# Seven half-size products in place of eight for 18 of 22 gate/up tiles of one SwiGLU sublayer

## The chip, the cores and the metric

The program runs on one core of one Trainium2 chip. The metric is the device time of one execution in microseconds; the kernel before takes 1680.61 us as the median of 3 runs (1678.48 to 1683.15). TensorE (PE) multiplies, VectorE (DVE), ScalarE (ACT) and GpSimd (POOL) work on what lies in the on-chip memories, and the queue of SyncE (SP) issues the loads.

## The reference

A two-layer backbone works on 256 latent tokens `x` and 256 context tokens `z`, with 1024 features. Each layer is a SwiGLU sublayer, a token mixer (a gated short convolution in layer 0, windowed attention in layer 1) and a second SwiGLU sublayer; all are in float32.

```python
def rmsnorm(x, g):
    y = x * lax.rsqrt(jnp.mean(x * x, axis=-1, keepdims=True) + RMS_EPS)
    return y * g

def swiglu(h, w_gu, w_down):                    # h [256, 1024], w_gu [1024, 2 * 2816], w_down [2816, 1024]
    gu = h @ w_gu
    return (jax.nn.silu(gu[..., :D_FF]) * gu[..., D_FF:]) @ w_down

def ffn_sublayer(x, mod, k, g_pre, g_post, w_gu, w_down):
    h = rmsnorm(x, g_pre) * (1 + mod[k + 1]) + mod[k]
    return x + 0.5 * mod[k + 2] * rmsnorm(swiglu(h, w_gu, w_down), g_post)

for i in range(2):
    mx = silu(c) @ w_mod[i] + b_mod[i]          # 9 vectors of 1024 coefficients; mz the same from c_ctx
    x = ffn_sublayer(x, mx, 0, ..., ffn_w_gu[i, 0], ffn_w_down[i, 0])
    z = ffn_sublayer(z, mz, 0, ..., ffn_w_gu[i, 0], ffn_w_down[i, 0])
    ...                                         # mixer, then the second SwiGLU sublayer
```

The change is in layer 1's first SwiGLU (`ffn_w_gu[1, 0]`), which both streams pass.

## The kernel before

The layout is feature-major: an activation is a row of tiles of 128 features by 512 tokens, the latent 256 tokens (slice `X`) in front of the context 256 (slice `Z`). A float32 product is carried by three fp32r products of split operands: each operand is cut into `hi` and `lo`, and hi*hi, lo*hi and hi*lo are summed in PSUM (L398, L399, L400, in `groups`). So each 128x128 weight tile costs three weight loads and three matmuls; a matmul streams 512 tokens ("128x512") or one stream's half of them ("128x256").

Weights come from DRAM in slots of 8 tiles, 128x1024 float32. `load` (L232 on) issues the slot's load on SP (L238) into a ring `raw` of 3 buffers, ACT copies it into `whi` (L243), and DVE, or POOL for the slots listed in `POOL`, subtracts to get `wlo` (L244). `whi` and `wlo` are rings of 8.

A SwiGLU sublayer (`ffn`) has 22 feature tiles, taken in three chunks. In a chunk, `gate_up` works out each feature tile: 8 weight tiles for gate and 8 for up, then ACT takes silu of gate (L436), DVE multiplies by up from PSUM (L438), and `hilo` splits the result into `ah` (ACT, L408) and `al` (DVE, L409). Then `project` multiplies the chunk's tiles by the down weights into `y` (8 output tiles; later chunks are added on DVE, L459). The first four tiles of the sublayer, the heads (`HEADS`), run for the latent half first and then for the context half, woven with the norms of the sublayer before; the norm chain of a half writes the new `h` as `hh` (ACT, L372) and `hl` (DVE, L373) from `ut` (DVE, L371, one input in PSUM).

The modulation vectors are worked out on DVE in between, as dots of 128x1024 (`dot`, L297) on weights that come through the same SP queue into two buffers `wmd`. The sublayer of the change carries 24 of them for one stream.

PE runs its instructions in the order of the program. The order on ACT, DVE, POOL and SP is set by a scheduler, and each engine takes its instructions in that order, so an instruction that waits holds all that stand behind it. The sublayer lies at about 961 to 1313 us of the profile.

Of the kernel before, what the change touches and what calls it, by code (L numbers as in the profile page):

```python
# [32 lines left out]
CHUNKS = {0: ((0, 7), (7, 14), (14, 22)), 2: ((0, 7), (7, 14), (14, 22)), 3: ((0, 7), (7, 14), (14, 22))}  # L33
# [5 lines left out]
# feature tiles of the first two adaLN chunks: by dots, by pairs; and the loads ahead of the first product (latent  # L39
# and context stream, tiles for dots, tiles of pairs, weights)  # L40
# [4 lines left out]
RAW = 3  # L45
# [52 lines left out]
def ffn_slots(w_gu, w_down, chunks):  # L98
# [3 lines left out]
    for a, b in chunks:  # L102
        out.append(slots_of(np.stack([gu[a:b], gu[FT + a:FT + b]], 1).reshape(-1, P, P)))
# [4 lines left out]
def lay_out(i):  # L108
# [9 lines left out]
    w += ffn_slots(i["ffn_w_gu"][1, 0], i["ffn_w_down"][1, 0], CHUNKS[3])  # L118
# [976 lines left out]
```

## Time and profile before

| | |
|---|---|
| median of 3 runs | 1680.61 us (1678.48 to 1683.15) |
| profiled execution, first to last instruction (its own time) | 1676.8 us |
| PE busy | 1642.4 us, 98% of the span |
| DVE, ACT, POOL busy | 1048.6, 644.0, 265.3 us |
| mean granted TensorE clock | 0.994 |
| DMA | 246.73 MB, mean 147 GB/s |

The profiled execution's own time is known only as its span, which lies 3.8 us below the median of the timed runs; the difference is what lies around the first and last instruction and between executions. PE's busy time is modelled from starts, so the pace of PE is better read from the starts of its matmuls. DVE's 63% is an average over stages that load it very differently.

### The profile page before, as it was taken

What the parts mean: (1) busy time and instruction counts of PE and PEld (TensorE: products, weight loads), DVE (VectorE), ACT (ScalarE), POOL (GpSimd) and SP (SyncE); (2) the same over time, 40 slices, a digit from 0 to 9 for tenths busy, and PEclk for the clock granted to TensorE, in tenths of its full rate; (3) what the DMA queues carried; (4) which work ended last, traced back from release to release, by engine and by line L of the source; (5) the groups of instructions that cost most, each with busy time, mean ns of one, the idle gap of its engine ahead of it and who ended that gap; (6) DMA issues with size and microseconds to landing.
All of it is one profiled execution on the core that took longest, in us unless ns stands there. A gap on an engine that the chain in (4) does not pass through costs nothing.

```text
span 1676.8 us, 23525 instructions
## 1 busy us (share of the span) xinstructions
PE 1642.4 (98%) x9378; PEld 1419.1 (85%) x9378; DVE 1048.6 (63%) x1570; ACT 644.0 (38%) x1051; POOL 265.3 (16%) x192
## 2 busy tenths in 40 slices
PE   8999999999999999999999999999999999989998
PEld 3788888889988998888888998888888997889987
DVE  7779779856644375977965564344443679665553
ACT  4532322325432643322232543222222558654442
POOL 1100000125102430000110521000000664130000
PEclk9999999999999999999999999999999999999999
DMA  8557556543322224655655224444433221045551
GB/s 317 188 164 237 189 187 217 194 156 102 101 89 101 68 71 165 213 188 165 219 191 166 80 74 148 160 132 150 153 124 114 94 89 64 26 160 198 194 192 50
DMA packets 70306, 246.73 MB, mean 147 GB/s; under 512 B 7730, under 2 KB 10290, under 8 KB 70196
## 3 DMA queue, kind: packets, MB, share of 16 engines
q1 hardware_dynamic: 69908, 245.02, 44.3%
q8 instruction: 73, 1.20, 0.3%
q14 instruction: 37, 0.30, 0.1%
q10 hardware_dynamic: 288, 0.20, 0.0%
HBM read 244.15 MB, written 1.05 MB: 146 GB/s over the span
## 4 chain that ended last, share of the span: by engine, by line
PE 90%; DVE 5%; ACT 2%; POOL 1%; issue 1%; DMA 1%; SPq 0%; DVEq 0%; POOLq 0%; ACTq 0%
PE mm L399 27%; PE mm L398 27%; PE mm L400 27%; PE mm L925 1%; PE mm L926 1%; PE mm L924 1%; PE po L801 1%; DVE junk L297 1%; PE tp L787 1%; POOL acc L359 1%; PE mm L747 1%; DMA xr<-in_xz 1%; PE prb L318 0%; ACT whi L243 0%; DVE acc L360 0%
## 5 line engine op out<-in xcount | busy, mean ns | idle before, releaser
L398 PE MATMUL mm<-hh,whi 128*128 128x512 f32 (+1 forms) x1520 | 549.3, 361 | 4.3 <-ACT hh L408 4.0
L399 PE MATMUL mm<-hh,wlo 128*128 128x512 f32 (+1 forms) x1520 | 547.9, 360 | 0.0
L400 PE MATMUL mm<-hl,whi 128*128 128x512 f32 (+1 forms) x1520 | 543.1, 357 | 0.0
L243 ACT ACTIVATE whi<-raw 128x1024 fp32r<-128x1024 f32 x316 | 330.5, 1056 | 440.2 <-PE mm L400 372.4
L244 DVE TENSOR_TENSOR wlo<-raw,whi 128x1024 fp32r<-128x1024 f32 x260 | 325.8, 1261 | 203.3 <-ACT whi L243 202.2
L398 PEld LDWEIGHTS mm<-hh,whi 128*128 128x128 f32 x1520 | 285.8, 188 | 53.6 <-ACT hh L408 5.3
L400 PEld LDWEIGHTS mm<-hl,whi 128*128 128x128 f32 x1520 | 285.9, 188 | 45.0 <-DVE hl L409 0.6
L399 PEld LDWEIGHTS mm<-hh,wlo 128*128 128x128 f32 x1520 | 286.3, 188 | 41.3
L297 DVE CUSTOM_DVE_ANT_0 junk<-wmd,sc,vec 128x1024 bf16<-128x1024 f32 x232 | 304.7, 1313 | 17.0 <-DMA wmd<-in_wmd 13.2
L244 POOL TENSOR_TENSOR wlo<-raw,whi 128x1024 fp32r<-128x1024 f32 x56 | 140.1, 2507 | 1005.2 <-ACT whi L243 1001.5
L398 PE MATMUL mm<-ah,whi 128*128 128x256 f32 (+1 forms) x848 | 276.8, 326 | 0.0
L399 PE MATMUL mm<-ah,wlo 128*128 128x256 f32 (+1 forms) x848 | 276.0, 326 | 0.0
L400 PE MATMUL mm<-al,whi 128*128 128x256 f32 (+1 forms) x848 | 274.1, 323 | 0.0
L398 PEld LDWEIGHTS mm<-ah,whi 128*128 128x128 f32 x848 | 160.5, 189 | 14.9
L400 PEld LDWEIGHTS mm<-al,whi 128*128 128x128 f32 x848 | 160.5, 189 | 14.1
L399 PEld LDWEIGHTS mm<-ah,wlo 128*128 128x128 f32 x848 | 160.8, 190 | 12.7
L438 DVE TENSOR_TENSOR pr<-mm,sg 128x512 f32<-128x512 f32 (+1 forms) x96 | 56.1, 584 | 181.6 <-PE mm L400 127.5
L436 ACT ACTIVATE sg<-mm 128x512 f32<-128x512 f32 (+1 forms) x96 | 49.2, 513 | 301.7 <-PE mm L400 301.7
L399 PE MATMUL mm<-h,wlo 128*128 128x256 f32 x352 | 98.8, 281 | 0.0
L398 PE MATMUL mm<-h,whi 128*128 128x256 f32 x352 | 98.6, 280 | 0.0
L400 PE MATMUL mm<-h,whi 128*128 128x256 f32 x352 | 98.4, 280 | 0.0
L409 DVE TENSOR_TENSOR al<-pr,ah 128x512 fp32r<-128x512 f32 (+1 forms) x84 | 74.6, 888 | 13.3 <-ACT ah L408 13.2
(185 smaller groups left out, 1496.5 us busy)
## 6 DMA issues: line engine op xcount, KB each, us to landing
raw<-in_wst SPq DMA_DIRECT2D x316, 512.0 KB, 3.5
wmd<-in_wmd SPq DMA_DIRECT2D x140, 512.0 KB, 4.2
xr<-in_xz SPq DMA_DIRECT2D x2, 1024.0 KB, 9.8
wmq<-in_wmd SPq DMA_DIRECT2D x8, 256.0 KB, 7.8
out_y<-xt SPq DMA_DIRECT2D x3, 256.0 KB, 2.1
rtab<-in_cst SPq DMA_DIRECT2D x1, 512.0 KB, 3.6
out_y<-xt SPq DMA_DIRECT2D x2, 128.0 KB, 1.8
msk<-in_cst ACTq DMA_DIRECT2D x1, 192.0 KB, 4.0
```

The costliest lines, as they stand in the source:

```text
L243: nc.scalar.activation(hi, raw, AF.Copy)
L244: d = sub.tensor_tensor(lo, raw, hi.bitcast(F32), ALU.subtract)
L297: self.keep(self.nc.vector.tensor_tensor_reduce(junk, wt, self.sc[v], 1.0, b, ALU.mult, ALU.add, out))
L359: nc.gpsimd.tensor_tensor(acc, acc, sq, ALU.add)
L398: nc.tensor.matmul(pt[:, :n], whi, rhi[:, sl], start=i == 0, stop=False)
L399: nc.tensor.matmul(pt[:, :n], wlo, rhi[:, sl], start=False, stop=False)
L400: nc.tensor.matmul(pt[:, :n], whi, rlo[:, sl], start=False, stop=i == last)
L409: i = (sub or self.nc.vector).tensor_tensor(lo[:, sl], src, hi[:, sl].bitcast(F32), ALU.subtract)
L436: nc.scalar.activation(sg[:, :n], pg[:, :n], AF.Silu)
L438: self.keep(nc.vector.tensor_mul(pr[:, :n], pu[:, :n], sg[:, :n]))
L747: nc.tensor.matmul(sp[e], act[4 * p2 + 2 * jp + jj][x][rows[e], qs], kt[p2][w][rows[e], :], start=a == 0, stop=False)
L787: nc.tensor.transpose(tp[:, c * P:(c + 1) * P], pe[c][:, kc // 2, kc % 2 * P:(kc % 2 + 1) * P], self.ident)
```

## The change

In the sublayer `ffn(1, 0)`, index 3 of the lists, the chunks become 6, 8 and 8 tiles instead of 7, 7 and 8. Tiles 0 to 3 stay as they were; tiles 4 to 21 are taken by twos in the new method `pair`, nine pairs: one in chunk 0, four each in chunks 1 and 2. A pair takes the two feature tiles of gate and of up, and the first and second half of the 1024 input features, as a 2x2 block matrix of weights, and the latent and context streams as the other one; seven products of sums of blocks replace eight products of blocks. Each of the seven has 8 weight tiles and 256 tokens, so 24 matmuls of 128x256; a pair has 168 of these where two tiles had 96 of 128x512. PE's order is P1 of the next pair, P7 of this pair, P2 to P6 of the next pair.

The sums of weight blocks are made on DVE (`s3`, and three sums in place, 128x1024 each); each of the seven operands is split (`split`), the `lo` on DVE except for P4, P5 and P6 (`POOLED`), which go to POOL. The activation sums are made once, in `forms`, ahead of the first pair: `hh + hl` for the eight feature tiles (half on POOL), four combinations of 128x1024, and their splits. Three of them keep 3 of the 8 buffers of `whi` and `wlo` until the sublayer's last pair; the fourth overwrites the context half of `h[0]` to `h[3]`. `RAW` goes from 3 to 6, the ring `tmp` from 3 to 4.

```diff
-CHUNKS = {0: ((0, 7), (7, 14), (14, 22)), 2: ((0, 7), (7, 14), (14, 22)), 3: ((0, 7), (7, 14), (14, 22))}
+CHUNKS = {0: ((0, 7), (7, 14), (14, 22)), 2: ((0, 7), (7, 14), (14, 22)), 3: ((0, 6), (6, 14), (14, 22))}
+SEVEN = {3: 4}
+POOLED = (3, 4, 5)
-RAW = 3
+RAW = 6
...
+    def split(self, src, sub=None):
+        hi = self.ring.tile([P, SLOT * P], F32R, name="whi", tag="whi")
+        lo = self.ring.tile([P, SLOT * P], F32R, name="wlo", tag="wlo")
+        self.nc.scalar.activation(hi, src, AF.Copy)
+        (sub or self.nc.vector).tensor_tensor(lo, src, hi.bitcast(F32), ALU.subtract)
+        return hi, lo
...
+    def forms(self):
...
+        hf = self.cp.tile([P, KT, N], F32, name="hf", tag="y")
+        for k in (4, 0, 5, 1, 6, 2, 7, 3):
+            hi, lo = (t.bitcast(F32) for t in self.h[k])
+            (nc.gpsimd if k % 4 in (1, 3) else nc.vector).tensor_tensor(hf[:, k], hi, lo, ALU.add)
+        fx, fz, bx, bz = (hf[:, k:k + 4, h] for k in (0, 4) for h in (X, Z))
...
+        nc.vector.tensor_tensor(fx, fx, fz, ALU.subtract)
+        nc.vector.tensor_tensor(fz, bz, fz, ALU.subtract)
...
+    def pair(self, s, forms, act):
...
+        a11 = self.raw(s)
+        w = self.split(a11, gp(0))
+        ba = self.bank()
+        product(ba, w, b11, True)
+        yield
+        up = tmp("up", "tmp", bufs=4)
+        nc.scalar.activation(up, ba, AF.Copy)
+        a21 = self.raw(s + 1)
+        s3 = self.ring.tile([P, SLOT * P], F32, name="raw", tag="raw", bufs=RAW)
+        nc.vector.tensor_add(s3, a11, a21)
+        w = self.split(s3, gp(1))
+        a22 = self.raw(s + 2)
+        nc.vector.tensor_add(a21, a21, a22)
+        bb = self.bank()
+        product(bb, w, t3, True)
+        gz = tmp("gz", "tmp", bufs=4)
+        nc.scalar.activation(gz, bb, AF.Copy)
+        nc.vector.tensor_add(a11, a21, a11)
+        w = self.split(a11, gp(2))
+        product(ba, w, t2)
+        gx = tmp("gx", "sq")
+        nc.scalar.activation(gx, ba, AF.Copy)
+        a12 = self.raw(s + 3)
+        w = self.split(a12, gp(3))
+        bc = self.bank()
+        product(bc, w, b21, True)
+        nc.vector.tensor_add(up, up, bc)
+        w = self.split(a21, gp(4))
+        product(ba, w, t1)
+        nc.vector.tensor_add(gz, gz, ba)
+        nc.scalar.activation(gz, gz, AF.Silu, scale=-1.0)
+        w = self.split(a22, gp(5))
+        product(bb, w, t4)
+        nc.vector.tensor_add(gx, gx, bb)
+        nc.scalar.activation(gx, gx, AF.Silu, scale=-1.0)
+        nc.vector.tensor_add(a12, a11, a12)
+        w = self.split(a12, gp(6))
+        yield
+        product(ba, w, b22)
+        nc.vector.tensor_mul(up, up, gx)
+        nc.vector.tensor_mul(gz, gz, ba)
+        for m in range(2):
+            c = slice(m * S, (m + 1) * S)
+            for t, h in ((up, X), (gz, Z)):
+                hi, lo = act[m]
+                nc.scalar.activation(hi[:, h], t[:, c], AF.Copy)
+                nc.vector.tensor_tensor(lo[:, h], t[:, c], hi[:, h].bitcast(F32), ALU.subtract)
...
+            for m in range(max(m0, seven), nk, 2):
+                p = self.pair(base + 2 * m, forms, act[m:m + 2])
+                next(p)
+                for _ in last or ():
+                    pass
+                next(p)
+                last = p
+                pace(2 * PACE)
+            for _ in last or ():
+                pass
```

Outside the sublayer PE's order is the same. On ACT and DVE the order changes a little at the start of the program: on DVE two more weight splits now stand ahead of the first `hl` of tile 5 and three ahead of that of tile 7, and ACT's copies move up with them.

The first place is DVE in the norm chain of the context half, while the latent heads run. Before, from `hl` of feature tile 3 (`hl_7618`) to that of tile 7 (`hl_7626`):

```order
L373 SCALAR_TENSOR_TENSOR hl_7618<-ut,mod_0_1_5992,hh_7617 128x256
L371 SCALAR_TENSOR_TENSOR ut<-xr,mod_1_1_5687,prb 128x256 x2
L438 TENSOR_TENSOR pr<-mm,sg 128x256
L373 SCALAR_TENSOR_TENSOR hl_7620<-ut,mod_0_1_5992,hh_7619 128x256
L373 SCALAR_TENSOR_TENSOR hl_7622<-ut,mod_0_1_5992,hh_7621 128x256
L371 SCALAR_TENSOR_TENSOR ut<-xr,mod_1_1_5687,prb 128x256
L409 TENSOR_TENSOR al_8234<-pr,ah_8233 128x256
L371 SCALAR_TENSOR_TENSOR ut<-xr,mod_1_1_5687,prb 128x256
L373 SCALAR_TENSOR_TENSOR hl_7624<-ut,mod_0_1_5992,hh_7623 128x256
L373 SCALAR_TENSOR_TENSOR hl_7626<-ut,mod_0_1_5992,hh_7625 128x256
```

The same stretch of DVE in the changed kernel, where L398 is the line of `hl`, and L473 and L477 are lines of `forms`:

```order
L398 SCALAR_TENSOR_TENSOR hl_7618<-ut,mod_0_1_5992,hh_7617 128x256
L463 TENSOR_TENSOR pr<-mm,sg 128x256
L398 SCALAR_TENSOR_TENSOR hl_7620<-ut,mod_0_1_5992,hh_7619 128x256
L396 SCALAR_TENSOR_TENSOR ut<-xr,mod_1_1_5687,prb 128x256 x2
L473 TENSOR_TENSOR hf<-hh_7619,hl_7620 128x512
L434 TENSOR_TENSOR al_8234<-pr,ah_8233 128x256
L477 TENSOR_TENSOR hf<-hf 128x4x256
L398 SCALAR_TENSOR_TENSOR hl_7622<-ut,mod_0_1_5992,hh_7621 128x256
L398 SCALAR_TENSOR_TENSOR hl_7624<-ut,mod_0_1_5992,hh_7623 128x256
L396 SCALAR_TENSOR_TENSOR ut<-xr,mod_1_1_5687,prb 128x256
L473 TENSOR_TENSOR hf<-hh_7623,hl_7624 128x512
L398 SCALAR_TENSOR_TENSOR hl_7626<-ut,mod_0_1_5992,hh_7625 128x256
```

Sums of `forms` now stand between the rows of the chain (two more, of tiles 0 and 2, stand just above this piece), and the row at L477 waits for POOL's sums of tiles 1 and 3.

The second place is DVE at the end of chunk 0. Before, its last feature tile there (tile 6, `al_8240`), with the dots behind it (`mod_7_0` is the modulation vector that they fill):

```order
L438 TENSOR_TENSOR pr<-mm,sg 128x512
L244 TENSOR_TENSOR wlo<-raw,whi 128x1024
L409 TENSOR_TENSOR al_8240<-pr,ah_8239 128x512
L297 ISA junk,mod_7_0_8951<-wmd,sc_95,vec 128x1024
L297 ISA mod_7_0_8951 128x1
```

In the changed kernel, the end of chunk 0's one pair (tiles 4 and 5; L554 is the last product's gate, L560 the `al`):

```order
L543 TENSOR_TENSOR gz_8911<-gz_8911,mm_8848 128x512
L547 TENSOR_TENSOR gx_8942<-gx_8942,mm_8886 128x512
L553 TENSOR_TENSOR up_8873<-up_8873,gx_8942 128x512
L322 ISA junk_9277,mod1_7_0_9045<-wmd_9245,sc0_95,vec_79 128x1024
L322 ISA mod1_7_0_9045 128x1
L554 TENSOR_TENSOR gz_8911<-gz_8911,mm_8848 128x512
L560 TENSOR_TENSOR al4_8236<-up_8873,ah4_8235 128x256
L560 TENSOR_TENSOR al5_8238<-up_8873,ah5_8237 128x256
L322 ISA junk_9301,mod1_7_0_9045<-wmd_9275,sc0_95,vec_79 128x1024
L322 ISA mod1_7_0_9045 128x1
L254 TENSOR_TENSOR wlo_9223<-raw_9220,whi_9222 128x1024
L560 TENSOR_TENSOR al4_8236<-gz_8911,ah4_8235 128x256
```

One dot now stands between P7 and the product `gz*ba` that waits for it, and a dot and a weight split stand ahead of the context half's `al`.

The third place is DVE in chunk 1. Before, two tiles' worth of it (`al4`, `al5`):

```order
L438 TENSOR_TENSOR pr_9637<-mm_9574,sg_9635 128x512
L244 TENSOR_TENSOR wlo_9884<-raw_9881,whi_9883 128x1024
L409 TENSOR_TENSOR al4_9282<-pr_9637,ah4_9281 128x512
L297 ISA junk_9643,mod1_6_0_9430<-wmd_9569,sc0_95,vec_79 128x1024
L297 ISA mod1_6_0_9430 128x1
L244 TENSOR_TENSOR wlo_9917<-raw_9914,whi_9916 128x1024
L438 TENSOR_TENSOR pr_9709<-mm_9646,sg_9707 128x512
L244 TENSOR_TENSOR wlo_9950<-raw_9947,whi_9949 128x1024
L409 TENSOR_TENSOR al5_9284<-pr_9709,ah5_9283 128x512
```

In the changed kernel, from P7's operand of the chunk's first pair to the middle of the second pair:

```order
L549 TENSOR_TENSOR raw_9659<-raw_9523,raw_9659 128x1024
L523 TENSOR_TENSOR raw_9830<-raw_9761,raw_9828 128x1024
L554 TENSOR_TENSOR gz_9388<-gz_9388,mm_9325 128x512
L560 TENSOR_TENSOR al0_9304<-gz_9388,ah0_9303 128x256
L560 TENSOR_TENSOR al1_9306<-gz_9388,ah1_9305 128x256
L271 TENSOR_TENSOR wlo_9753<-raw_9659,whi_9752 128x1024
L526 TENSOR_TENSOR raw_9828<-raw_9828,raw_9836 128x1024
L271 TENSOR_TENSOR wlo_9764<-raw_9761,whi_9763 128x1024
L540 TENSOR_TENSOR up_9588<-up_9588,mm_9665 128x512
L531 TENSOR_TENSOR raw_9761<-raw_9828,raw_9761 128x1024
L271 TENSOR_TENSOR wlo_9833<-raw_9830,whi_9832 128x1024
L543 TENSOR_TENSOR gz_9626<-gz_9626,mm_9529 128x512
```

DVE's row now holds sums of weights (L523, L526, L531, L549) between the splits, and no dots in these pairs.

## Rows read from the trace of the kernel before

**Rows 1.** The page, busy time by engine (share of the span, instructions).

```profile
PE 1642.4 (98%) x9378; PEld 1419.1 (85%) x9378; DVE 1048.6 (63%) x1570; ACT 644.0 (38%) x1051; POOL 265.3 (16%) x192
```

**Rows 2.** Windows of chunks 1 and 2: busy us per engine, clock, DMA share, GB/s.

```profile
1079.10:1156.00 76.90, 76.90 (x338) 63.09 (x337) 29.89 (x35) 21.83 (x28) 0.00 (x0) 1.00 0.37 121
1194.40:1282.40 88.00, 88.00 (x386) 72.22 (x385) 37.13 (x42) 24.47 (x31) 2.42 (x1) 1.00 0.43 137
```

**Rows 3.** Timeline of PE, chunk 1: start, duration, matmul; first and last of 336.

```profile
1079.41 0.39 PE L398 MATMUL mm<-hh,whi 128*128 128x512 f32 x1
...
1156.10 0.39 PE L400 MATMUL mm<-hl,whi 128*128 128x512 f32 x1
```

**Rows 4.** Timeline of PE, heads of the context half: first and last of 54 matmuls.

```profile
984.33 0.28 PE L398 MATMUL mm<-hh,whi 128*128 128x256 f32 x1
...
990.57 0.28 PE L400 MATMUL mm<-hl,whi 128*128 128x256 f32 x1
```

**Rows 5.** Timeline of PE, down products in 545 to 560: first and last of 135.

```profile
544.78 0.28 PE L400 MATMUL mm<-al,whi 128*128 128x256 f32 x1
...
559.96 0.28 PE L399 MATMUL mm<-ah,wlo 128*128 128x256 f32 x1
```

**Rows 6.** Groups by shape in 1007.7 to 1282.4: count, busy us, mean ns, idle before.

```profile
L244 DVE TENSOR_TENSOR wlo<-raw,whi 128x1024 fp32r<-128x1024 f32 x48 | 58.8, 1225 | 93.0 <-ACT whi L243 93.0
L243 ACT ACTIVATE whi<-raw 128x1024 fp32r<-128x1024 f32 x51 | 53.9, 1057 | 108.2 <-PE mm L400 96.1 <-issue 11.9
L297 DVE CUSTOM_DVE_ANT_0 junk<-wmd,sc,vec 128x1024 bf16<-128x1024 f32 x23 | 29.4, 1279 | 4.3 <-DMA wmd<-in_wmd 4.2
L244 POOL TENSOR_TENSOR wlo<-raw,whi 128x1024 fp32r<-128x1024 f32 x4 | 10.0, 2500 | 237.5 <-ACT whi L243 237.5
```

**Rows 7.** Timeline of POOL and DVE in 823 to 829.

```profile
825.05 2.91 POOL L244 TENSOR_TENSOR wlo<-raw,whi 128x1024 fp32r<-128x1024 f32 x1 [178.38 <-ACT whi L243]
...
824.40 1.28 DVE L297 CUSTOM_DVE_ANT_0 junk<-wmd,sc,vec 128x1024 bf16<-128x1024 f32 x1
...
825.61 0.68 DVE L459 TENSOR_TENSOR y<-y,mm 128x512 f32<-128x512 f32 x1
826.54 2.51 DVE L297 CUSTOM_DVE_ANT_0 junk<-wmd,sc,vec 128x1024 bf16<-128x1024 f32 x1 [0.24 <-DMA wmd<-in_wmd]
```

**Rows 8.** Timeline of PE, its longest wait before a product.

```profile
53.13 0.79 PE L398 MATMUL mm<-hh,whi 128*128 128x512 f32 x1 [4.04 <-ACT hh L408]
```

**Rows 9.** Timeline of DVE, the context half's norm chain.

```profile
984.20 0.87 DVE L373 SCALAR_TENSOR_TENSOR hl<-ut,mod,hh 128x256 fp32r<-128x256 f32 x2 [0.15 <-ACT hh L372]
...
988.63 0.48 DVE L373 SCALAR_TENSOR_TENSOR hl<-ut,mod,hh 128x256 fp32r<-128x256 f32 x1 [0.16 <-ACT hh L372]
```

**Rows 10.** Groups of POOL over the span: its 128x512 sums.

```profile
L359 POOL TENSOR_TENSOR acc<-acc,sq 128x512 f32<-128x512 f32 x16 | 27.4, 1714 | 17.8 <-ACT sq L357 17.6
```

**Rows 11.** Timeline of DVE and PE where chunk 1 ends and its down products begin.

```profile
1156.32 0.39 PE L398 MATMUL mm<-ah,whi 128*128 128x512 f32 x1
...
1156.52 0.69 DVE L438 TENSOR_TENSOR pr<-mm,sg 128x512 f32<-128x512 f32 x1 [2.63 <-PE mm L400]
1157.62 1.22 DVE L244 TENSOR_TENSOR wlo<-raw,whi 128x1024 fp32r<-128x1024 f32 x1 [0.40 <-ACT whi L243]
1158.76 0.68 DVE L409 TENSOR_TENSOR al<-pr,ah 128x512 fp32r<-128x512 f32 x1
```

**Rows 12.** Timeline of PE behind a wait in a norm.

```profile
952.43 0.87 PE L318 MATMUL prb<-mean,acc 128*128 128x1 f32 x4 [1.98 <-DVE acc L361]
...
953.52 0.41 PE L399 MATMUL mm<-ah,wlo 128*128 128x256 f32 x1
...
955.87 0.34 PE L398 MATMUL mm<-ah,whi 128*128 128x256 f32 x1
```

**Rows 13.** The page, loads: count, KB each, us from issue to landing.

```profile
raw<-in_wst SPq DMA_DIRECT2D x316, 512.0 KB, 3.5
wmd<-in_wmd SPq DMA_DIRECT2D x140, 512.0 KB, 4.2
```

More of the change, by code (lines that the diff above doesn't have):

```diff
@@ L95, in halves_of, with ffn_slots @@
     return w.reshape(k // 2, 2, P, 2, 512).transpose(3, 0, 2, 1, 4).reshape(k, P, D)
-def ffn_slots(w_gu, w_down, chunks):
+def ffn_slots(w_gu, w_down, chunks, seven=FT):
     gu = tiles_of(w_gu)
@@ L102, in ffn_slots @@
     for a, b in chunks:
-        out.append(slots_of(np.stack([gu[a:b], gu[FT + a:FT + b]], 1).reshape(-1, P, P)))
+        c = min(max(a, seven), b)
+        if a < c:
+            out.append(slots_of(np.stack([gu[a:c], gu[FT + a:FT + c]], 1).reshape(-1, P, P)))
+        for m in range(c, b, 2):
+            for f, k in ((FT, 0), (0, 0), (0, 4), (FT, 4)):
+                out.append(slots_of(gu[f + m:f + m + 2, k:k + 4].reshape(-1, P, P)))
         out.append(slots_of(dn[:, a:b].reshape(-1, P, P)))
@@ L117, in lay_out @@
     w += ffn_slots(i["ffn_w_gu"][0, 1], i["ffn_w_down"][0, 1], CHUNKS[2])
-    w += ffn_slots(i["ffn_w_gu"][1, 0], i["ffn_w_down"][1, 0], CHUNKS[3])
+    w += ffn_slots(i["ffn_w_gu"][1, 0], i["ffn_w_down"][1, 0], CHUNKS[3], SEVEN[3])
     qkv = i["attn_w_qkv"][0]
@@ L246, in load, with raw @@
             self.keep(d)
+        return hi, lo
+    def raw(self, s):
+        assert s == self.slot_at, (s, self.slot_at)
+        self.slot_at += 1
+        raw = self.ring.tile([P, SLOT * P], F32, name="raw", tag="raw", bufs=RAW)
+        self.nc.sync.dma_start(out=raw, in_=self.a["wst"][s])
+        return raw
+    def split(self, src, sub=None):
[3 more added lines that the diff above has]
+        (sub or self.nc.vector).tensor_tensor(lo, src, hi.bitcast(F32), ALU.subtract)
         return hi, lo
@@ new lines, in pair, with product @@
+    def pair(self, s, forms, act):
+        nc = self.nc
+        b11, t3, t2, b21, t1, t4, b22 = forms
+        gp = lambda i: nc.gpsimd if i in POOLED else None
+        def product(bank, w, rhs, first=False):
+            hi, lo = w
+            for m in range(2):
+                out = bank[:, m * S:(m + 1) * S]
+                for k in range(4):
+                    c = slice((4 * m + k) * P, (4 * m + k + 1) * P)
+                    rh, rl = rhs[k]
+                    mm = lambda w, r, start=False, stop=False: nc.tensor.matmul(out, w, r, start=start, stop=stop, skip_group_check=True)
+                    mm(hi[:, c], rh, start=first and m == 0 and k == 0)
+                    mm(lo[:, c], rh)
+                    mm(hi[:, c], rl, stop=k == 3)
+        tmp = lambda name, tag, **kw: self.wk.tile([P, N], F32, name=name, tag=tag, **kw)
+        a11 = self.raw(s)
[39 more added lines that the diff above has]
+        nc.vector.tensor_mul(gz, gz, ba)
+        for m in range(2):
+            c = slice(m * S, (m + 1) * S)
[3 more added lines that the diff above has]
+                nc.vector.tensor_tensor(lo[:, h], t[:, c], hi[:, h].bitcast(F32), ALU.subtract)
@@ L501, in ffn @@
         pace = self.pacer(nmods, PACE * (22 - m0) + 16)
+        forms = None
         for ci, (a, b) in enumerate(CHUNKS[3 * l + j]):
@@ L515, in ffn @@
                     next(start, None)
-            for m in range(m0, nk):
+            seven = SEVEN.get(3 * l + j, FT) - a
+            for m in range(m0, min(nk, seven)):
                 self.weave([self.gate_up(ALL, base, [m], act)])
                 pace(PACE)
+            if 3 * l + j in SEVEN and forms is None:
+                forms = self.forms()
+            last = None
+            for m in range(max(m0, seven), nk, 2):
[8 more added lines that the diff above has]
+                pass
             base += 2 * nk
@@ L593, in mix @@
             nh = n // S
-            cs = self.wk.tile([P, N], F32, name="sg", tag="tmp", bufs=3)
+            cs = self.wk.tile([P, N], F32, name="sg", tag="tmp", bufs=4)
             nc.scalar.activation(cs[:, :n], cg[:, :n], AF.Copy)
@@ L599, in mix @@
             nc.vector.tensor_mul(cu[:, :, 1:S + 1], v3(u), v3(cs))
-            t = self.wk.tile([P, N], F32, name="pr", tag="tmp", bufs=3)
+            t = self.wk.tile([P, N], F32, name="pr", tag="tmp", bufs=4)
             nc.scalar.activation(v3(t), cu[:, :, 0:S], AF.Identity, scale=self.cw(0, m))
@@ L639, in attention @@
         nc.scalar.dma_start(out=msk, in_=self.a["cst"][:, 4 * S:])
-        rot = wk.tile([P, P], F32, name="rot", tag="tmp", bufs=3)
+        rot = wk.tile([P, P], F32, name="rot", tag="tmp", bufs=4)
         nc.scalar.activation(rot, msk[:, 0:P], AF.Copy)
-        mib = wk.tile([P, 3 * P], BF16, name="mib", tag="tmp", bufs=3)
+        mib = wk.tile([P, 3 * P], BF16, name="mib", tag="tmp", bufs=4)
         mkb, idb = mib[:, :2 * P], mib[:, 2 * P:]
@@ L657, in rope @@
             else:
-                t, u = (lambda w: (w[:, 0], w[:, 1]))(wk.tile([P, 2, S], F32, name="t1", tag="tmp", bufs=3))
+                t, u = (lambda w: (w[:, 0], w[:, 1]))(wk.tile([P, 2, S], F32, name="t1", tag="tmp", bufs=4))
             nc.scalar.activation(t, p[:, X], AF.Copy)
@@ L1032, in turn @@
         def turn(p):
-            row = self.wk.tile([2, N], F32, name="row", tag="tmp", bufs=3)
+            row = self.wk.tile([2, N], F32, name="row", tag="tmp", bufs=4)
             nc.scalar.activation(row, sums[p][0:2, :], AF.Copy)
@@ L1089 @@
     arrays = lay_out({k: np.asarray(v) for k, v in inputs.items()})
[L1090 removed]
+    nc = bacc.Bacc("TRN2", target_bir_lowering=False, num_devices=1, dynamic_dma_scratch_size=1024)
     build(nc, {n: v.shape for n, v in arrays.items()})
```

22 lines of the change are left out of this document (19 added, 3 removed).

## The prediction

> **What bounds the kernel now.** I read first the busy times by engine, then the windows of the changed stage, then the starts of PE's matmuls. PE is busy 98% of the span [rows 1], and in the windows of chunks 1 and 2 it is busy for the whole window at clock 1.00, while DVE works 29.9 of 76.9 us and 37.1 of 88.0 us and POOL hardly at all [rows 2]. So here PE's stream of matmuls sets the time, and the question is whether the engines that feed it, with far more to do, stay hidden.
>
> The pace comes from starts, since a matmul's listed duration overlaps the next. 336 matmuls of 128x512 lie between 1079.41 and 1156.10: 76.69 / 335 = 228.9 ns each, without a gap [rows 3]. With 128x256, 54 lie between 984.33 and 990.57: 6.24 / 53 = 117.7 ns [rows 4]. Half the tokens cost a little more than half the time.
>
> **PE's share of the change.** A pair of tiles takes 96 x 228.9 ns = 21.97 us before and 168 x 117.7 ns = 19.78 after, 2.2 us less; nine pairs give 19.7. One stretch shows 128x256 at 15.18 / 134 = 113.3 ns [rows 5], which would make it 9 x (21.97 - 19.03) = 26.5. I take 117.7, because it stands in the same stage and for the same `hh`/`hl` operands, and keep 26.5 as a bound.
>
> Beside this term stands a rule of the Trainium skill ("TensorE: Matmul & The Clock Gate", section "Back-to-back issue gap"): an isolated matmul costs its columns at 2.4 GHz plus about 2.5 ns, but in a stream the weight loads belong to the spacing too. By the isolated form, as an estimate, a pair would save 96 x 215.8 - 168 x 109.2 ns = 2.4 us, 21 us in all; the rows here lie some 8 to 13 ns above that form, and the sum goes by the rows.
>
> **DVE and POOL in a pair.** DVE gets 4 sums of 128x1024 and 4 splits (8 x 1.225 us, [rows 6]), one 128x512 with both inputs in SBUF (0.68, [rows 11]) and four `al` of 128x256 (0.43 each, half of a pair of `hl`, [rows 9]): 12.2 us. Instructions that follow directly start about 0.08 before the end of the one ahead (the split of 1157.62 ends at 1158.84, its successor starts at 1158.76, [rows 11]), so 11.2. Four more read PSUM: 4 x 0.69 = 2.8 [rows 11]. POOL gets three splits of 2.5: 7.5 [rows 6]. These do not simply lie side by side. A dot that started 1.5 us into POOL's split took 2.51 instead of 1.28 and ended 1.09 us after the split, while a sum from PSUM in the middle of the same split took its usual 0.68 [rows 7]. So DVE with two SBUF inputs and POOL take turns, and DVE with a PSUM input does not wait. A pair then needs 11.2 + 7.5 = 18.7 us if all PSUM work lies beside POOL, and 21.5 if none does, against PE's 19.8.
>
> That alone stops nothing: five of eight ring slots stay free, so a split can run four products of 2.83 us, 11 us, ahead of its use; its place behind sums that wait for PE leaves about 7. At 21.5 a chunk of four pairs loses 3 x 1.7 = 5 us of that lead. Chunk 2 has about seven dots, 7 x 1.36 = 9.5 us, so there up to 5 + 9.5 - 7 = 7.5 us could reach PE; at 18.7 nothing does. Between 0 and 7.5 I take **+1.5**, near the lower end: one PSUM row stands beside a POOL split in the trace, and it was not held. ACT has 7 x 1.057 us and about 5 us of small work, 12.4 of 19.8, and stays hidden. DMA brings the same four slots a pair at a load share of 0.37 to 0.43 [rows 2].
>
> **The context half's heads.** `hl` of tile 7 ended at 988.63 + 0.48 = 989.11 [rows 9], and PE first needed it at 990.57 [rows 4]: 1.5 us of cover. DVE now does four sums of 128x512 (0.68) and one combination of 1.225 ahead of it, less overlaps 3.5 us; and the combination waits for POOL's sum of tile 3, 1.7 us with its holds [rows 10]. The stall is 3.5 - 1.5 = 2.0 without POOL, 3.7 with it, 4.5 if POOL's next sum comes between as well: **+3.2**. The rest of `forms` has some 14 us before the first pair needs it, about what it takes.
>
> **The first pair and the end of chunk 0.** P7 needs `ba` back from the sum behind P5, which stands behind two dots whose loads wait on SP behind raw slots; 4.2 us of landing [rows 13] puts it 1 us ahead of its need. Then comes the tight place. After P7, the down product reaches tile 4 after four tiles x 3 x 0.229 = 2.75 us and its `al` 0.46 later, 3.2. Until then DVE must do, behind a dot that may just have begun, `gz*ba` 0.69, two `al` 0.86, dot 1.36, split 1.22, `al` 0.43: 4.6, up to 5.9. That is 1.4 to 2.7 late, and POOL's splits of the down weights can put 2.5 between once or twice. I take **+3**, of 1.4 to 7.5.
>
> **The ends of chunks 1 and 2.** Before, DVE's last `al` ended at 1159.44, and the eighth tile was needed at 1156.32 + 7 x 0.687 = 1161.1 [rows 11]. Now two tiles and both halves end together; the seventh is needed at 4.6 us after P7 against `gz*ba` 0.69, an ACT copy 0.4 behind a split of 1.06, a DVE split 1.22, `al` 0.43 = 3.8, or 6.3 with a POOL hold. **+1** for both (0 to 3.4).
>
> **The start.** PE waited 4.04 us for `hh` there [rows 8]. Two or three more splits of 1.06 (ACT) and 1.22 (DVE) now stand ahead of the last `hh` and `hl`; their data may be late or on time, 0 to 3: **+1.6**.
>
> **The clock.** After a wait of 1.98 us PE's matmuls of 128x256 ran at 213 ns, its 1.2 GHz level, from 953.52 to 955.87 [rows 12]: 11 steps in 2.35 us, which at 117.7 ns would be 1.29, so 1.1 us lost on top of the wait. The two new stalls (heads, chunk 0) can each bring this, 0 to 2.4 in all: **+1.2**.
>
> **The sum.** -19.7 + 1.5 + 3.2 + 3 + 1 + 1.6 + 1.2 = **-8.2 us**. Against the profiled execution, 1676.8, that is a span of 1668.6. The median of the timed runs lies 3.8 above the profiled span, and so I predict **1672.4 us**.
>
> **Rivals.**
> All hidden. The new chains run ahead and PE shows only its gain: -19.7 and perhaps 1 to 2 back, **1662**; with 113.3 ns, 1654. For it: nearly every cover is within 3 us of enough. Against: the in-order rows in the norm chain leave no way round 2 us there.
>
> The costs eat it. The first stretch goes to its upper ends: heads 4.5, chunk 0 7.5, clock 2.4, the start 3, ends 1: -19.7 + 18.4 = -1.3, **1679**. For it: the dots and POOL's splits do stand there. Against: it needs most of them late at once.
>
> Slower, by the loop of raw buffers and POOL. A pair's fourth load can only be issued when POOL has finished the last split of the pair before; then landing, ACT's copy, and three POOL splits, each of which may first wait for a DVE instruction: 3.5 + 1.06 + 3 x (2.5 + 1.22) = 15.7 us, under 19.8. If each split waits for two DVE instructions and a modulation load stands ahead in SP's order (4.2), it is 3.5 + 1.06 + 3 x (2.5 + 2.45) + 4.2 = 23.6: 3.8 a pair over PE, for eight pairs 30, less 7 of lead in each chunk, 16 beyond the forecast: **1688**. It decides above about 22 us a pair. Against: loads run ahead, and DVE often waits for PE.
> The Trainium skill ("SBUF — State Buffer", section "SBUF: two separate sides") calls the port of DVE and GpSimd a lock that its holder keeps for a whole instruction, and by that rule POOL adds no capacity beside DVE's two-input work. The dot of 2.51 us agrees.
>
> **How the numbers follow.** The forecast 0.48 (own range 1667 to 1677), all hidden 0.16, eaten 0.18, slower 0.18. What a measurement can tell from no change is 0.3%, 5 us: below 1675.6 is faster. The forecast's case lies almost wholly there, and I give faster 0.63, same 0.18, slower 0.19. The range reaches from all hidden to just short of the slower rival: 1660 to 1686.
>
> **What would show it.** PE's matmuls in the pairs start 117.7 ns apart, 168 a pair, 19.8 us from P1 to P1. A wait on `hl` in 985 to 995 of 2 to 4 us. A wait on `al` or `ah` at the first down product of chunk 0. In chunks 1 and 2 DVE and POOL together near 19 us a pair with PE unbroken. The prediction is wrong if 128x256 runs at another pace with these operands, if PE waits for `wlo` in every pair, or if the heads' stall is absent.

## The result and the profile after

The changed kernel is slower: 1692.74 us as the median of 8 runs against 1680.58 of 8 runs of the kernel before, a ratio of 1.0068 with an interval of 1.0045 to 1.0091. The prediction was 1672.4, with a range that ended at 1686. One timed run of the rings alone (2317 us, granted clock 0.65) and one without the pair in chunk 0 (1793 us, 0.85) were disturbed and are left out of the medians below.

The profiled execution spans 1688.5 us, 11.7 more than before. The page, busy time by engine, beside [rows 1]:

```profile
PE 1633.4 (97%) x10026; PEld 1441.0 (85%) x10026; DVE 1160.3 (69%) x1667; ACT 691.8 (41%) x1130; POOL 342.9 (20%) x222
```

PE has less to do, by 9 us of modelled time, and DVE has 112 us more, POOL 78. What PE saved is to be seen in chunk 1, which runs without a wait. Timeline of PE, first and last of its 672 matmuls, beside [rows 3]:

```profile
1084.48 0.28 PE L508 MATMUL mm<-hh,whi 128*128 128x256 f32 x1
...
1164.20 0.28 PE L508 MATMUL mm<-hl,whi 128*128 128x256 f32 x1
```

79.72 / 671 = 118.8 ns a step, 19.96 us a pair, where two tiles took 21.97: 2.0 us each, and 18.1 for nine if all went at this pace. So the arithmetic pays. The loss is elsewhere. Windows of the heads, of the first pair, of chunk 1 and of chunk 2 (columns as in [rows 2]):

```profile
961.00:1019.10 58.10, 55.53 (x452) 54.55 (x451) 47.65 (x85) 26.98 (x53) 18.11 (x14) 0.97 0.12 39
1019.10:1047.40 28.30, 21.83 (x169) 21.42 (x168) 21.44 (x18) 11.32 (x15) 19.65 (x7) 0.88 0.56 205
1084.20:1164.10 79.90, 79.90 (x673) 79.82 (x673) 64.08 (x60) 43.48 (x61) 28.50 (x11) 1.00 0.40 126
1208.20:1296.70 88.50, 83.28 (x674) 82.64 (x673) 81.28 (x78) 45.48 (x63) 33.11 (x12) 0.96 0.47 159
```

The one pair of chunk 0 takes 28.4 us instead of 20, and the four of chunk 2 take 88.4 instead of 79.8; DVE is busy there 81.3 of 88.5 us. All nine take 196.7 us, where the 18 tiles took 197.7: the gain of the arithmetic is spent inside the pairs. The waits of PE in 961 to 1300 (total, times, longest) name what came late:

```profile
PE mm L508 <- DVE gz L543: 7.4, 2, 5.7
PE mm L508 <- ACT gx L535: 4.3, 2, 3.5
PE mm L425 <- DVE hl L398: 2.4, 2, 1.8
PE mm L425 <- DVE al L560: 2.0, 1, 2.0
PE mm L423 <- ACT hh L397: 0.2, 1, 0.2
```

Before, PE had no wait between the heads and the tail of this stage. The longest is P7 of chunk 0's pair. Timeline of PE, DVE, SP and POOL ahead of it:

```profile
1043.27 0.58 PE L508 MATMUL mm<-hh,whi 128*128 128x256 f32 x1 [5.70 <-DVE gz L543]
...
1026.55 3.42 DVE L549 TENSOR_TENSOR raw<-raw 128x1024 f32<-128x1024 f32 x1
1029.89 1.27 DVE L322 CUSTOM_DVE_ANT_0 junk<-wmd,sc,vec 128x1024 bf16<-128x1024 f32 x1
...
1031.20 1.28 DVE L322 CUSTOM_DVE_ANT_0 junk<-wmd,sc,vec 128x1024 bf16<-128x1024 f32 x1
...
1033.55 0.68 DVE L540 TENSOR_TENSOR up<-up,mm 128x512 f32<-128x512 f32 x1
1037.20 2.12 DVE L322 CUSTOM_DVE_ANT_0 junk<-wmd,sc,vec 128x1024 bf16<-128x1024 f32 x1 [2.97 <-DMA wmd<-in_wmd]
...
1039.37 3.23 DVE L322 CUSTOM_DVE_ANT_0 junk<-wmd,sc,vec 128x1024 bf16<-128x1024 f32 x1
...
1042.54 0.68 DVE L543 TENSOR_TENSOR gz<-gz,mm 128x512 f32<-128x512 f32 x1
...
1031.19 1.66 SPq L292 DMA_DIRECT2D wmd<-in_wmd  x2
...
1032.57 8.96 POOL L254 TENSOR_TENSOR wlo<-raw,whi 128x1024 fp32r<-128x1024 f32 x3 [3.68 <-ACT whi L253]
```

Read it from the end. The sum `gz += ba` (L543), which gives `ba` back to P7, runs in its usual 0.68 us, but only from 1042.54. Ahead of it in DVE's queue stand two dots. The first waited 2.97 us for its load, issued only at 1031.19; then both were held by POOL's three splits in a row and took 2.12 and 3.23 us instead of 1.28. PE waited 5.70 us meanwhile. Why the load was late is in SP's waits in 1010 to 1050:

```profile
SPq L292 <- DVE mod L322: 22.0, 6, 10.2
```

The loads of `wmd` wait for earlier dots to give one of the two buffers back, here for the dot of 1029.89. That dot stood behind a weight sum (L549) of 3.42 us instead of 1.22, which was itself held: POOL ran three splits from 1020.57 to 1028.88.

In chunk 2 the way is longer. Timeline of PE, DVE, POOL and ACT there:

```profile
1245.21 0.58 PE L508 MATMUL mm<-hh,whi 128*128 128x256 f32 x1 [3.52 <-ACT gx L535]
...
1234.41 0.67 DVE L547 TENSOR_TENSOR gx<-gx,mm 128x512 f32<-128x512 f32 x1
1235.01 2.84 DVE L322 CUSTOM_DVE_ANT_0 junk<-wmd,sc,vec 128x1024 bf16<-128x1024 f32 x1
...
1237.78 3.42 DVE L549 TENSOR_TENSOR raw<-raw 128x1024 f32<-128x1024 f32 x1
...
1241.20 0.68 DVE L553 TENSOR_TENSOR up<-up,gx 128x512 f32<-128x512 f32 x1
...
1230.41 9.70 POOL L271 TENSOR_TENSOR wlo<-raw,whi 128x1024 fp32r<-128x1024 f32 x3 [14.93 <-ACT whi L270]
...
1241.91 0.72 ACT L559 ACTIVATE ah<-up 128x256 fp32r<-128x256 f32 x2 [5.21 <-DVE up L553]
...
1244.58 0.58 ACT L535 ACTIVATE gx<-mm 128x512 f32<-128x512 f32 x1
```

DVE's dot and its weight sum are both held by POOL (2.84 and 3.42 us); `up*gx` is late behind them; ACT's first instruction waits 5.21 us for it, and the copy of `gx` that empties PE's bank stands behind that. The Trainium skill ("SBUF — State Buffer", section "SBUF: two separate sides") says that a GpSimd instruction which reads SBUF and a DVE instruction with two SBUF inputs exclude each other for the whole instruction. The trace agrees: the two sums from PSUM that start while POOL is busy, at 1234.41 here and at 1033.55 in the first pair, keep 0.67 and 0.68 us.

Each long wait also cost clock. Windows of PE at these two waits and, in the middle row, around the wait of 2.0 us for `al` (length, PE's busy time, granted clock, DMA share, GB/s; 0.50 is the 1.2 GHz level):

```profile
1043.20:1046.50 3.30, 3.23 (x15) 0.50 0.82 285
1050.20:1056.00 5.80, 3.78 (x12) 0.77 0.87 335
1243.50:1250.20 6.70, 4.99 (x23) 0.57 0.24 82
```

Behind 5.70 and 3.52 us of wait PE ran at half pace for some 3 and 5 us, which costs half of each again. Over the nine pairs, 196.7 us less 11.7 of waits less 1512 steps of 118.8 ns leave 5.4 us for it.

A part lies outside the stage. The norm ahead of it, beside [rows 12]:

```profile
960.03 0.58 PE L343 MATMUL prb<-mean,acc 128*128 128x1 f32 x4 [3.66 <-DVE acc L386]
```

That instruction started at 952.43 before: the changed kernel reached the stage 7.6 us late. Only 1.7 of them arise at this wait, by the starts of the same instructions in both traces; 4.8 were there by 386 us. Of these, 2.2 arise between 21 and 25 us, where PE's granted clock from 20 to 27 us is 0.58, against 1.00 before; the fastest version below shows 0.56 there, so the wide rings need not be the cause. Of the 11.7 us between the two traces, 7.9 are lost before 989 us, 6.2 from there to the stage's end and 2.8 in the norms behind it; some 5 are won back after that.

### The profile page after: what moved, and what is told of

It is laid out like the page before. It is cut to its first block, busy times and chain, and to the rows that moved or that the text cites. A ratio compares the mean times of both kernels' runs of the same rounds, so it can differ in the third digit from the quotient of the medians.

```text
span 1688.5 us, 24981 instructions
## 1 busy us (share of the span) xinstructions
PE 1633.4 (97%) x10026; PEld 1441.0 (85%) x10026; DVE 1160.3 (69%) x1667; ACT 691.8 (41%) x1130; POOL 342.9 (20%) x222
## 3 DMA queue, kind: packets, MB, share of 16 engines
q8 instruction: 78, 1.28, 0.3%
## 4 chain that ended last, share of the span: by engine, by line
PE 85%; DVE 7%; issue 2%; ACT 2%; POOL 2%; DMA 1%; SPq 0%; DVEq 0%; ACTq 0%; POOLq 0%
PE mm L423 23%; PE mm L425 23%; PE mm L424 23%; PE mm L508 8%; DVE junk L322 2%; PE po L937 1%; PE mm L1062 1%; PE mm L1061 1%; PE mm L1060 1%; POOL acc L384 1%; DMA wmd<-in_wmd 1%; PE tp L923 1%; PE mm L883 1%; DMA xr<-in_xz 1%; PE prb L343 0%
## 5 line engine op out<-in xcount | busy, mean ns | idle before, releaser
L423 PE MATMUL mm<-hh,whi 128*128 128x512 f32 (+1 forms) x1232 | 438.3, 356 | 5.4 <-ACT hh L433 5.0
L253 ACT ACTIVATE whi<-raw 128x1024 fp32r<-128x1024 f32 x280 | 291.9, 1056 | 352.4 <-PE mm L425 289.2
L425 PE MATMUL mm<-hl,whi 128*128 128x512 f32 (+1 forms) x1232 | 433.0, 351 | 3.1 <-DVE hl L398 2.4
L424 PE MATMUL mm<-hh,wlo 128*128 128x512 f32 (+1 forms) x1232 | 432.1, 351 | 0.0
L254 DVE TENSOR_TENSOR wlo<-raw,whi 128x1024 fp32r<-128x1024 f32 x225 | 289.4, 1297 | 109.9 <-ACT whi L253 108.6
L254 POOL TENSOR_TENSOR wlo<-raw,whi 128x1024 fp32r<-128x1024 f32 x55 | 140.3, 2557 | 758.4 <-ACT whi L253 758.3
L423 PEld LDWEIGHTS mm<-hh,whi 128*128 128x128 f32 x1232 | 231.9, 188 | 39.5 <-ACT hh L433 6.3
L425 PEld LDWEIGHTS mm<-hl,whi 128*128 128x128 f32 x1232 | 231.8, 188 | 38.7 <-DVE hl L398 2.8
L424 PEld LDWEIGHTS mm<-hh,wlo 128*128 128x128 f32 x1232 | 232.2, 189 | 31.9 <-POOL wlo L254 0.2
L425 PEld LDWEIGHTS mm<-al,whi 128*128 128x128 f32 x848 | 161.5, 190 | 16.7 <-DVE al L560 2.4
L423 PEld LDWEIGHTS mm<-ah,whi 128*128 128x128 f32 x848 | 161.5, 190 | 13.8
L463 DVE TENSOR_TENSOR pr<-mm,sg 128x512 f32<-128x512 f32 (+1 forms) x78 | 43.6, 560 | 125.1 <-PE mm L425 81.8
L271 POOL TENSOR_TENSOR wlo<-raw,whi 128x1024 fp32r<-128x1024 f32 x27 | 72.4, 2693 | 191.7 <-ACT whi L270 189.1
```

Source lines behind the costliest of these rows:

```text
L253: nc.scalar.activation(hi, raw, AF.Copy)
L254: d = sub.tensor_tensor(lo, raw, hi.bitcast(F32), ALU.subtract)
L271: (sub or self.nc.vector).tensor_tensor(lo, src, hi.bitcast(F32), ALU.subtract)
L423: nc.tensor.matmul(pt[:, :n], whi, rhi[:, sl], start=i == 0, stop=False)
L424: nc.tensor.matmul(pt[:, :n], wlo, rhi[:, sl], start=False, stop=False)
L425: nc.tensor.matmul(pt[:, :n], whi, rlo[:, sl], start=False, stop=i == last)
```

## The experiments

Each line of medians stands beside the kernel before on the same chip (1679.2 us for the first four, 1680.3 for the next four, 1680.6 for the last three); differences between medians of different groups carry what these differ by, up to 1.4 us. Theory W, formed on the trace above: PE's gain is real, and the loss is made of waits, because dots and other instructions that wait stand in DVE's queue ahead of the sums that free PE's banks. Its rivals are the shared port alone (P), the wider rings (R) and the mere amount of extra work (L).

**The rings alone.** The kernel before with the three sizes that the change sets: six raw slots, four buffers of `tmp`, and a scratch of 1024 for DMA descriptors, which the section on the change does not name:

```diff
-RAW = 3
+RAW = 6
...
-            sg = self.wk.tile([P, N], F32, name="sg", tag="tmp", bufs=3)
+            sg = self.wk.tile([P, N], F32, name="sg", tag="tmp", bufs=4)
```

> The kernel before with the changed ring sizes alone (raw 6, tmp 4, the smaller scratch for descriptors), no block products. Theory W (the loss comes from waits of PE inside the stage, because dots and their loads stand ahead of the sums that free PE's banks): the rings only shift the order elsewhere, 2 to 5 us slower than before, 1683 to 1686 us, since PE reached the changed stage 7.6 us later in the changed kernel and about 2.4 us were given back behind it. Rival R (the ring sizes and the order that follows from them are the loss): 1690 us or more. If the shift was chance of two executions: 1680 to 1681.

Measured 1685.82, ratio 1.0041 (1.0023 to 1.0059): the upper end of theory W's range, and a good half of the whole loss without any block product. Its waits of PE in 900 to 1400 show two of the places:

```profile
PE prb L318 <- DVE acc L361: 7.4, 3, 3.7
PE prb L328 <- POOL rr L322: 3.4, 1, 3.4
```

The longest wait for `acc` was 2.7 before and that for `rr` 0.4; the three waits for `acc` together were 7.3, so there one grew and another shrank. A third place is the start, where PE waits 5.0 us for `hh` instead of 4.0, and 0.9 for `hl`. With these sizes the scheduler sets weight splits ahead of the steps of a norm. Timeline of DVE ahead of the wait of 3.7 us for `acc`, before and with the rings:

```profile
948.73 1.55 DVE L244 TENSOR_TENSOR wlo<-raw,whi 128x1024 fp32r<-128x1024 f32 x1 [0.39 <-ACT whi L243]
950.20 1.22 DVE L360 TENSOR_TENSOR acc<-acc,sq 128x512 f32<-128x512 f32 x1
...
950.56 3.22 DVE L244 TENSOR_TENSOR wlo<-raw,whi 128x1024 fp32r<-128x1024 f32 x2 [0.40 <-ACT whi L243]
...
954.04 0.88 DVE L360 TENSOR_TENSOR acc<-acc,sq 128x512 f32<-128x512 f32 x1
```

**Dots out of the pairs.** The dots are paced over the down products, and the pairs' sums and `al` keep the program's order:

```diff
-        pace = self.pacer(nmods, PACE * (22 - m0) + 16)
+        pace = self.pacer(nmods, 16 if 3 * l + j in SEVEN else PACE * (22 - m0) + 16)
...
-                pace(2 * PACE)
...
-        nc.vector.tensor_add(gz, gz, ba)
+        self.keep(nc.vector.tensor_add(gz, gz, ba))
```

> The changed kernel with the 24 dots of the stage moved out of the pairs to the down products, the pairs' output sums on DVE kept in the order of the program. Theory W: the waits at P7 of the first pair (5.7 us), at the first down product (2.0) and in chunk 2 (1.7 and 3.5) go, and with them about 5 us of half clock: 1672 to 1680 us. Rival P (POOL's three splits per pair hold DVE through the shared port, with or without dots): most waits stay, 1687 to 1693 us.

Measured 1676.07, ratio 0.9973 (0.9954 to 0.9991): theory W. The work is the same and 16.7 us are gone. Two things changed at once, the place of the dots and the order of the sums; the run with the order alone, below, separates them. The longest waits that PE still has in the stage are

```profile
PE mm L425 <- DVE hl L398: 1.8, 1, 1.8
PE mm L508 <- DVE gz L543: 1.6, 1, 1.6
PE mm L423 <- ACT ah L559: 0.8, 1, 0.8
```

**No pair in chunk 0.**

```diff
-SEVEN = {3: 4}
+SEVEN = {3: 6}
```

> The changed kernel with tiles 4 and 5 as plain tiles: eight pairs, none in chunk 0. Theory W: the first pair's waits (0.8, 5.7, 2.0) and their half clock (about 3.5) go, 2 us of PE's gain are given up: about 1683 us. Rival (the dots only wait for another pair, and the same wait shows in chunk 1): 1689 to 1693 us.

Measured 1680.67, ratio 1.0001 (0.9984 to 1.0018). Theory W again, 2 us better than expected: the first pair cost 12 us net. The wait of 3.5 us for `gx` in chunk 2 stayed.

**No split of a pair on POOL.**

```diff
-POOLED = (3, 4, 5)
+POOLED = ()
```

> The changed kernel with all seven splits of a pair on DVE, none on POOL (the down slots that go to POOL stay there). Theory W: dots and their loads still stand ahead of the sums, so most of the waits stay: 1686 to 1692 us. Rival P: 7.5 us of POOL per pair are replaced by 3.7 on DVE and the holds go: 1676 to 1684 us. If DVE's own queue is the limit: 1695 us or more.

Measured 1678.97, ratio 0.9989 (0.9970 to 1.0009): rival P, against what theory W had expected. DVE has 3.7 us more a pair, and the kernel is 13.8 us faster. PE waits 6.6 us inside the stage, against 16.3 in the changed kernel (the trace is of the slowest execution, 1689.85 us, whose loss lies ahead of the stage). So neither the dots nor POOL is the cause alone: either one taken away removes most of the waits.

**Rings apart.** The raw ring is cut in two of three, and only the pairs use the second:

```diff
-RAW = 6
+RAW = 3
...
-        a21 = self.raw(s + 1)
-        s3 = self.ring.tile([P, SLOT * P], F32, name="raw", tag="raw", bufs=RAW)
+        a21 = self.raw(s + 1, "rawb")
+        s3 = self.ring.tile([P, SLOT * P], F32, name="raw", tag="rawb", bufs=RAW)
...
-        a12 = self.raw(s + 3)
+        a12 = self.raw(s + 3, "rawb")
```

> The changed kernel with the ring of raw slots cut in two rings of three, one of which only the pairs use, so that the rest of the program sees three buffers as before (the ring tmp stays at four). Theory W: what the wide ring costs elsewhere, 6.9 us in the run with the rings alone, comes back and the stage keeps its waits: 1684 to 1688 us. Rival (the pairs need a ring of six, and two of three bring new waits on loads): 1692 us or more.

Measured 1688.19, ratio 1.0052 (1.0036 to 1.0067), just above theory W's range: 4.6 of the expected 6.9 by the medians, and the interval meets that of the changed kernel, so this run alone does not show the ring's price. The longest wait for `acc` is back to 2.6, but the stage takes 2.8 us more (335.8 us from 984.1, against 333.0 from 988.8). Its waits moved from one bank to another:

```profile
PE mm L508 <- DVE gz L543: 9.3, 3, 5.0
PE mm L508 <- ACT gx L535: 2.5, 3, 1.1
```

Their total in the stage is 16.4 us, 16.3 in the changed kernel.

**Dots out and no split on POOL.** The two edits together.

> The changed kernel with the dots moved to the down products and kept in order, and with no split of a pair on POOL. If dots and POOL's holds make the same waits together (theory W and P both in part): 1671 to 1675 us, little under the 1676 of the dots alone. If each has waits of its own, the gains add, 16 and 13 us: about 1663 us.

Measured 1673.88, ratio 0.9963 (0.9949 to 0.9977): little under the dots alone. In the trace PE has no wait left in any pair. The two make the same waits together, as the trace of P7 shows, where dots stand at the head of the queue and POOL holds them.

**The same with the rings apart.**

> The run before it in this list (dots out, no split on POOL) with the two rings of three. Theory W: 5 to 7 us less than that run, 1665 to 1669 us. Rival (the ring's price was one of the stage): no difference to that run.

Measured 1665.30, ratio 0.9924 (0.9909 to 0.9938): 8.6 us less, theory W and a little more. In a stage without the other waits the ring's price comes back in full; of the three sizes only the raw ring's differs between these two versions.

**And the norm chain free.** The eight sums of `forms` on DVE, tile 7 first, kept in that order, so that they cannot stand between the context half's `hl`:

```diff
-        for k in (4, 0, 5, 1, 6, 2, 7, 3):
+        for k in (7, 3, 6, 2, 5, 1, 4, 0):
             hi, lo = (t.bitcast(F32) for t in self.h[k])
-            (nc.gpsimd if k % 4 in (1, 3) else nc.vector).tensor_tensor(hf[:, k], hi, lo, ALU.add)
+            self.tc.stamp_issue_order_token(nc.vector.tensor_tensor(hf[:, k], hi, lo, ALU.add).ins, "forms")
```

> The same with the eight sums of the forms all on DVE and in the order 7, 3, 6, 2, 5, 1, 4, 0, which puts them behind the context half's last hl, so that the norm chain stands on DVE as in the kernel before. By my term for the heads, 3.2 us predicted and 3.6 to 4.2 measured, another 3 to 4 us go: 1662 to 1665 us. Rival (the forms are late for the first pair instead): the wait moves to the second or third product and the time stays within 1 us of the run before it.

Measured 1664.31, ratio 0.9912 (0.9896 to 0.9927), the fastest of all, 16 us below the kernel before. The wait of 2.4 us on `hl` is gone and did not move to the first pair; what PE still waits for in 955 to 1300 is, above all,

```profile
PE prb L343 <- DVE acc L386: 2.0, 1, 2.0
PE mm L425 <- DVE al L560: 1.3, 2, 0.8
PE mm L423 <- ACT ah L559: 0.6, 1, 0.6
```

The step of 1.0 us in the medians is less than the 3 to 4 expected, and the intervals of the two runs overlap, so the size of this term is shown by the traces and not by the times: from the wait for `acc` ahead of the stage to the next norm's first product they have 342.23 us without this edit (from 952.39) and 338.55 with it (from 955.47), 3.7 less.

**Order alone.** The changed kernel with `keep` on the pairs' sums and `al`, everything else as it was:

> The changed kernel with one difference: the pairs' output sums and the al on DVE are kept in the order of the program, so that the dots, with the pace of the changed kernel, stand behind them in the first pair and singly in the later ones. Theory W (what costs is a dot, waiting for its load or held by POOL, at the head of DVE's queue in front of a sum that frees a bank): the waits of chunk 0 go, those of chunk 2 shrink, 1677 to 1683 us. Rival L (the dots' work and loads as such crowd the stage, wherever they stand): 1688 us or more.

Measured 1681.44, ratio 1.0003 (0.9987 to 1.0019): theory W by the time, and rival L falls. The same dots and loads lie in the stage; they only stand behind the sums. Timeline of DVE in the first pair:

```profile
1032.63 0.69 DVE L543 TENSOR_TENSOR gz<-gz,mm 128x512 f32<-128x512 f32 x1 [2.21 <-PE mm L508]
1035.44 0.69 DVE L547 TENSOR_TENSOR gx<-gx,mm 128x512 f32<-128x512 f32 x1 [2.13 <-PE mm L508]
1036.05 1.28 DVE L322 CUSTOM_DVE_ANT_0 junk<-wmd,sc,vec 128x1024 bf16<-128x1024 f32 x1
```

Now DVE waits for PE, and P7 waits for nothing. The dots out of the pairs, as in the second run, give 5.4 us more in the medians. In chunk 2 theory W had expected the waits to shrink, and they hardly do: 4.9 us in all, where the changed kernel has 5.2.

```profile
PE mm L508 <- ACT gx L535: 2.6, 2, 2.3
PE mm L508 <- DVE gz L543: 2.3, 1, 2.3
```

**The dots put back into the fastest version.**

> The fastest version so far (two rings, no split of a pair on POOL, norm chain free) with the dots put back where the scheduler sets them in the changed kernel. If dots and POOL's holds make the waits only together: 1664 to 1668 us. If the dots have waits of their own: 1671 us or more.

Measured 1668.30, ratio 0.9928 (0.9905 to 0.9951), 4.0 us more in the medians, just above the range for waits that are made only together; the intervals still meet. Without POOL's splits the dots cost little.

**POOL's splits put back into the fastest version.**

> The fastest version so far with P4, P5 and P6 of each pair split on POOL again, dots still out of the pairs. If POOL's holds make waits only together with the dots: 1664 to 1667 us. If they have waits of their own, as the 2 us between the two runs with the dots out suggest: 1666 to 1670 us.

Measured 1674.02, ratio 0.9962 (0.9943 to 0.9980): a miss of both ranges, 9.7 us more than without in the medians (8.4 by the ratios). So in narrow rings POOL's splits have waits of their own. The longest is again one of a bank, in chunk 2's last pair. In the list of PE's waits:

```profile
PE mm L508 <- DVE gz L543: 4.7, 1, 4.7
```

and in the timeline of DVE and ACT:

```profile
1269.10 1.23 DVE L254 TENSOR_TENSOR wlo<-raw,whi 128x1024 fp32r<-128x1024 f32 x1 [3.10 <-ACT whi L253]
1270.24 0.68 DVE L543 TENSOR_TENSOR gz<-gz,mm 128x512 f32<-128x512 f32 x1
...
1268.01 1.06 ACT L253 ACTIVATE whi<-raw 128x1024 fp32r<-128x1024 f32 x1 [4.34 <-DMA raw<-in_wst]
```

A split of down weights, waiting for ACT and that for a late load, stands ahead of the sum. That the load was late because POOL gave the slot back late is my reading and was not tried by itself.

**All traces together.** Counted from their first product to the down products, the pairs tell two causes apart. Chunk 0's pair takes 28.4 and 26.0 us in the two versions with dots ahead of the sums and splits on POOL, 20.9 and 21.4 where only POOL's splits are gone, and 19.9 or 20.0 in all six that keep the sums in order, on POOL or not. The four pairs of chunk 2 take 79.7 us in all five versions without POOL's splits, and 81.6 to 91.1 in the six with them, whatever the order. So at the first pair the order alone is enough; in chunk 2 it is not, and no version with POOL's splits is free of waits there.

## Why the prediction was wrong

**The step that failed** is the one on the first pair: "P7 needs `ba` back from the sum behind P5, which stands behind two dots whose loads wait on SP behind raw slots; 4.2 us of landing [rows 13] puts it 1 us ahead of its need." So the wait for `ba` stood in the sum with nothing. The dots ahead of the sum were read rightly and their time wrongly: I took dots of 1.28 us and loads on time. The loads waited in the end for their buffers and not for raw slots, the dots were 2.12 and 3.23 us long, the first began 2.97 us late, and the sum came 5.7 us after its need. With the waits of 2.0 us behind it (for `al`) and 0.8 ahead of it (for `gx`), chunk 0 lost 8.5 us of waits where I had 3, and my bound of 7.5 was for another place in it. The runs confirm it from two sides: without the pair 12 us come back, and with the same work in another order 11.3.

That is not the whole miss. Between the forecast of -8.2 us and the 11.7 of the traces lie 19.9: 16.0 in the stage (-9.8 forecast, 6.2 measured), in chunk 0, chunk 2 and the half clock behind their waits, and 3.9 outside it (1.6 forecast, 5.5 measured).

**PE's gain**: 19.7 forecast, 18.1 at the pace measured in chunk 1, since a matmul took 118.8 ns and not 117.7. A small miss of size.

**DVE and POOL in a pair**: +1.5 for both chunks, from 0 to 7.5. Chunk 1 had no wait, as reckoned; chunk 2 lost 1.7 and 3.5. The reckoning by lead was right for the weights, which came in time. It left out that the same held queue also carries the sums that free the banks, and these have no lead: one product after P5 the bank is wanted. That is the second step that failed.

**The heads**: +3.2, and waits of 2.4 on `hl` were there for the reason given; taking the sums out of the chain removed them.

**The ends of chunks 1 and 2**: +1, and no wait was there.

**The start**: +1.6 for a few moved splits, and the waits there grew by 1.7 (5.0 for `hh` instead of 4.0, and 0.7 for `hl`). I had seen that the order moved and had priced it at this one place, and the section on the change says that outside the sublayer it moves only there; but the rings move it at norms too. The rings alone cost 6.9 us by the ratio.

**The clock**: +1.2. The mechanism was right; with 5.7 and 3.5 us of wait it was about half of 3.3 and of 5.0 us of busy time, 1.6 and 2.5, at these two places, and more behind the wait of 2.0. The two stalls that I had priced were those of the heads and of chunk 0.

**The rivals.** The slower one, 1688, came nearest in number, by luck: it named the loop of raw buffers and POOL, and no wait for `wlo` shows, so it was not this. POOL was in it, but as the one who holds DVE. That the costs eat the gain, 1679, was nearest in mechanism, and it still held the first pair and the rings too cheap. All hidden, 1662, is near what the change can give: the version with order, port and rings put right runs at 1664.3.

## What to carry to other kernels

A sum that gives a PSUM bank back is as urgent as the weights, and has no lead: look in an in-order queue for what can wait ahead of it (a load, another engine, the shared port), and price that instruction with its wait, not with its bare duration. A helper engine behind a shared port need not be extra capacity: here three splits of 2.5 us on POOL cost more than the same three on DVE at 1.2. A wider ring for one stage can move the order of the whole program; here a ring of its own for the stage took the price back. Compare the order far from the change as well.

## What the runs showed of the hardware that was not expected

The same kind of matmul has two paces without any wait. The last sublayer's 1056 products of 128x256 are the same in all versions; in the profiled execution of the changed kernel they took about 5 us less than before, 113.6 instead of 118.4 ns from start to start. The version with the rings apart has 113.5, all others 117.9 to 118.7. A stretch at 545 us goes the other way, 113.3 before [rows 5] and 117.8 after, and the products with the stored forms ran at 120.0. No experiment here tells what sets it; a few us of the differences between versions may lie in it.
